# A two-layer hybrid decoder trunk on one core: first weights in halves, warm-up products, squares straight into the ones product, paired output transfers and a new order of issue

## The chip, the cores and the metric

The kernel runs on one core of a Trainium2 chip. Its engines are TensorE (PE; its weight loads are shown as PEld), VectorE (DVE), ScalarE (ACT), GpSimd (POOL) and SyncE (SP), which issues nearly all transfers. The metric is device time in microseconds, the median of the runs of a kernel; lower is better.

## The reference

Two layers. In each, an RMSNorm, one input projection whose columns go to four mixers, an RMSNorm for each mixer's output, an output projection and a residual; then an RMSNorm, a gated FFN and a residual. At the end a last RMSNorm. Everything is float32, the sequence is 1024 long and the model 1024 wide, the FFN 2816.

```python
for l in range(DEPTH):
    h = rmsnorm(x, attn_norm[l])
    proj = h @ w_in[l]
    (c_q, c_kv, k_r, g_b, g_c, u_conv, u_pool,
     q_sw, k_sw, v_sw) = jnp.split(proj, pts, axis=-1)
    y_a = mla_attention(...)        # causal, latent, 4 heads
    y_b = short_gated_conv(...)     # width 3
    y_c = multiscale_pool(...)      # windows 2, 4, 8, 16
    y_d = swa_sink_attention(...)   # window 128, ALiBi, sinks
    groups = jnp.stack([y_a, y_b, y_c, y_d], axis=2)
    gf = groups.astype(jnp.float32)
    gf = gf * lax.rsqrt(jnp.mean(gf * gf, axis=-1, keepdims=True) + RMS_EPS)
    mixed = (gf.reshape(b, s, D_MIX) * mix_norm[l]).astype(x.dtype)
    x = x + mixed @ w_o[l]
    h2 = rmsnorm(x, ffn_norm[l])
    gate, up = jnp.split(h2 @ w_gate_up[l], 2, axis=-1)
    x = x + (jax.nn.silu(gate) * up) @ w_down[l]
return rmsnorm(x, final_norm)
```

## The kernel before

**Layout.** Activations are kept transposed: eight tiles `d` of 128 model channels on the partitions, two halves `t` of 512 positions on the free axis. Every product is made from operands that are split in two: a high part, cast to float32r (`act.copy`, L215 for weights, L283 and L286 elsewhere), and a low part, the rest (`dve.tensor_tensor` with subtract, L216, L284, L287). `mm3` (L272 is its product) adds high by high, high by low and low by high into one PSUM bank, so an output of 128 by 512 over 1024 channels is 24 products. Plain float32 is left in the transposes (L560, L950) and in products with a tile of ones (L336); one with ones is two passes in the trace.

**Stages.** For each layer: the projections of `w_in` and the four mixers with their attention, the output projection, the gate and up products with a Strassen-like scheme over blocks of two by two (`gu_start`, `onto`; `snap`, L1176, copies a partial sum from PSUM between two products onto the same bank; 21 such tiles a layer and one plain one), then the down products in seven combinations of blocks (`B11` to `B22`). In the profile attention and projections of layer 0 are about 50 to 450 us, its FFN 450 to 1050, and the same again for layer 1 until 2008.

**The start.** SP first loads the first weights `w_in[0, 2]`, 128 by 1024 (L207 in `weights`), then in `enter` (L366) the eight tiles of x of one half and later the second weights and the other half. POOL loads `par`, all gains and small parameters (L131). `enter` scales each x tile by its gain on ACT while splitting it (L286, `pcol` reads `par`), and DVE makes the low part (L287). `enter_norm` adds up the squares (`SumSq.add`: Square on ACT, L318, addition on DVE, L324). DVE writes `ones` first of all (L135).

**The end.** In the last layer the block `B22` is done for two column ranges, 0 to 256 and 256 to 512, of the second half of positions; `tail` holds its four accumulations. After each, `evac` adds the bank to x on DVE (L1575), `ss.add` squares and adds it, with the last addition also adding the epsilon (L320). `rnorm` sums over partitions with a product with ones (L336) and takes the inverse root on ACT and DVE (L338 to L344). `finish` scales the eight tiles by gain and norm on DVE (L380) and sends each (L384).

**The order of issue.** `steps_of` makes a list of steps from the program, with what each waits for and its duration in a table of costs. `places` gives each group of instructions its rank plus a shift from the table `MOVES`; `arrange` runs a planner over the list: each engine takes, of what is ready by `SIGNAL` (from the end of a step on one engine until another may use it) and has a buffer that is free (its last use's end and 40 ns), the step of the lowest place. `order_engines` binds the instructions of every engine, SP's transfers too, to the order that comes out.

Of the kernel before, what the change touches and what calls it, by code (L numbers as in the profile page):

```python
# [18 lines left out]
P = 128  # L19
# [92 lines left out]
def trunk_kernel(ctx: ExitStack, tc: tile.TileContext, ins, out):  # L112
# [13 lines left out]
    def rd(ap):  # L126
        return ap.bitcast(F32)


    par = cpool.tile([P, L * PC_N + NK], F32, name="par")  # L130
    pool.dma_start(par, ins["params"])  # L131
# [50 lines left out]

    def tmp(tag="te"):
        return tpool.tile([P, HT], F32, name=tag, tag=tag, bufs={"te": 2, "tn": 3, "tp": 3}[tag])
# [18 lines left out]
    def weights(src, n):  # L203
        if n > 2 * P:
            s = F.pair()
            raw = F.ap2(s)
            sp.dma_start(raw[:, :n], src)  # L207
# [7 lines left out]
        act.copy(hi[:, :n], raw[:, :n])  # L215
        dve.tensor_tensor(out=lo[:, :n], in0=raw[:, :n], in1=rd(hi[:, :n]), op=ALU.subtract)  # L216
# [81 lines left out]
    class SumSq:  # L298
# [7 lines left out]
        def add(self, t, f, cols=whole):  # L306
# [12 lines left out]
            if m == self.n // P:  # L319
# [6 lines left out]
        def rnorm(self, t, cols=whole, tag="t", parts=False):  # L326
# [8 lines left out]
            else:  # L335
                pe.matmul(p, ones, a, start=True, stop=True)  # L336
# [24 lines left out]

    def enter(t):

        for k in range(NK):
            s = xf[k][t] = F.half()
            sp.dma_start(F.ap(s), x_in[k, :, t * HT : (t + 1) * HT])  # L366
            hh[k][t] = half_split(F.ap(s), pcol(0, PC_ATTN + k))

    def enter_norm(t):
# [3 lines left out]
        ratt[t] = ss.rnorm(t, parts=True)  # L373

# [10 lines left out]

    last_silu = None
    for l in range(L):
# [1251 lines left out]
        for cols in (slice(0, 256), slice(256, HT)) if last else ():  # L1639
            for m, p, w in tail:  # L1640
# [64 lines left out]
DRAM_TILES = {"xs", "xp", "xr", "qd", "out"} | {f"ad{n}" for n in range(7)}  # L1705
# [112 lines left out]
def arrange(steps, rank=lambda v: v.rank):  # L1818
# [29 lines left out]
    def takes(v, t):  # L1848
        for name in (x for x in v.tiles if x not in live):
            tag = name.rsplit("_", 1)[0]  # L1850
            if queue[tag][0] != name or tag in held_by or not freed[tag] or freed[tag][0] + 40 > t:
                return False
        return True

    while any(now.values()) or any(later.values()):
# [23 lines left out]
        for name in (x for x in v.tiles if x not in live):  # L1879
# [5 lines left out]
            if freed[tag][0] + 40 > t:  # L1885
                wait = max(wait or 0, freed[tag][0] + 40)
# [289 lines left out]
```

## Time and profile before

| what | value |
|---|---|
| time, median of 3 runs | 2057.77 us (2057.12 to 2057.89) |
| the profiled execution's own time | 2056.9 us |
| its span (first to last instruction) | 2055.1 us |
| PE busy | 2031.7 us (99%) |
| PEld, DVE, ACT busy | 1669.6, 1616.3, 991.3 us |
| moved by DMA | 289.74 MB, 141 GB/s in the mean |

A busy TensorE is not one at its peak: its products are pipelined and the ends are modelled, so the pace of products and the waits of the weight loads say more than the busy share. A row of a timeline gives the start and length in us, engine, line, operation, what is written from what, and how many; a bracket gives the idle time ahead of it and what ended it. A row of waits gives who waited for whom: us in total, times, longest. A row of a landing gives a transfer's size and the us from issue to landing.

### The profile page before, as it was taken

Reading aid. Unit: us, or ns where it says so; the run is one execution under the profiler, and the core shown is the slowest. Engines: PE = TensorE matmul, PEld = TensorE weight load, DVE = VectorE, ACT = ScalarE, POOL = GpSimd, SP = SyncE. Lnnn points to the kernel's source line nnn. Section 1 sums busy time; section 2 is a strip of 40 time slices with the busy share of each in tenths; the row PEclk is TensorE's granted clock in tenths of the full one; section 3 lists DMA queues with packets and bytes.
Section 4 is the critical chain, followed back from the end, with each engine's and each line's share of the span. In section 5 each row is a group of like instructions: output and inputs, shape, how many; then the busy total and the mean of one; then the engine's idle time right before and its main releaser. Section 6 shows DMA issues by size and latency. Waiting matters only on the chain.

```text
span 2055.1 us, 26087 instructions
## 1 busy us (share of the span) xinstructions
PE 2031.7 (99%) x9394; PEld 1669.6 (81%) x9394; DVE 1616.3 (79%) x2872; ACT 991.3 (48%) x1738; POOL 6.7 (0%) x37
## 2 busy tenths in 40 slices
PE   8999999999999999999999999999999999999997
PEld 6887787888888888888888877888788888888887
DVE  7888988997887878655666898889987787786555
ACT  7447657653333335444443576667433333355342
POOL 0000000000000000000000000000000000000000
PEclk9999999999999999999999999999999999999999
DMA  4110222344544447866401102232553444497552
GB/s 182 34 52 31 74 97 86 135 142 161 188 145 170 161 145 259 297 212 207 147 36 44 47 14 90 94 104 97 185 186 139 165 172 144 154 317 271 196 178 83
DMA packets 148817, 289.74 MB, mean 141 GB/s; under 512 B 12608, under 2 KB 72000, under 8 KB 148688
## 3 DMA queue, kind: packets, MB, share of 16 engines
q1 hardware_dynamic: 148656, 288.03, 40.5%
q8 instruction: 74, 1.21, 0.2%
q14 instruction: 55, 0.45, 0.1%
q0 software_dynamic: 32, 0.04, 0.0%
HBM read 204.66 MB, written 83.36 MB: 140 GB/s over the span
## 4 chain that ended last, share of the span: by engine, by line
PE 92%; DVE 3%; ACT 2%; DMA 1%; issue 1%; SPq 0%; DVEq 0%; ACTq 0%
PE ps_mm L272 36%; PE ps_s L272 29%; PE ps_t L272 11%; PE ps_pv L272 8%; PE ps_pv L962 1%; PE ps_t L950 1%; PE ps_s L896 1%; PE ps_t L336 1%; PE ps_pv L572 1%; PE ps_s L898 1%; PE ps_s L897 1%; DMA u<-in_w_o 1%; PE ps_s L511 1%; PE ps_mm L770 1%; DVE u L324 1%
## 5 line engine op out<-in xcount | busy, mean ns | idle before, releaser
L272 PE MATMUL ps_mm<-u,u 128*128 128x512 f32 (+1 forms) x3426 | 855.2, 390 | 10.6 <-ACT u L286 7.2
L272 PEld LDWEIGHTS ps_mm<-u,u 128*128 128x128 f32 x3426 | 629.0, 189 | 140.6 <-ACT u L286 7.2
L272 PE MATMUL ps_s<-u,u 128*128 128x512 f32 x2676 | 646.5, 390 | 0.4 <-ACT u L283 0.4
L272 PEld LDWEIGHTS ps_s<-u,u 128*128 128x128 f32 x2676 | 501.1, 188 | 107.8 <-ACT tn L1176 1.9
L283 ACT CAST u<-u 128x1024 fp32r<-128x1024 f32 (+2 forms) x388 | 335.9, 889 | 392.6 <-PE ps_s L272 85.6
L284 DVE TENSOR_TENSOR u<-u,u 128x1024 fp32r<-128x1024 f32 (+2 forms) x388 | 389.4, 1020 | 148.2 <-ACT u L283 122.4
L272 PE MATMUL ps_t<-u,u 128*128 128x512 f32 (+1 forms) x1118 | 265.3, 378 | 0.0
L272 PEld LDWEIGHTS ps_t<-u,u 128*128 128x128 f32 x1118 | 202.7, 188 | 39.0 <-issue 0.5
L272 PE MATMUL ps_pv<-u,u 128*128 128x512 f32 x696 | 172.0, 390 | 0.0
L272 PEld LDWEIGHTS ps_pv<-u,u 128*128 128x128 f32 x696 | 130.3, 188 | 27.9 <-ACT tn L1176 0.6
L1316 ACT ACTIVATE tp<-tp 128x512 f32<-128x512 f32 x84 | 53.0, 632 | 146.7 <-DVE tp L348 146.5
L283 ACT CAST u<-ps_t 128x512 fp32r<-128x512 f32 (+4 forms) x136 | 64.8, 506 | 73.7 <-PE ps_t L560 35.6
L286 ACT ACTIVATE u<-u,par 128x512 fp32r<-128x512 f32 x100 | 69.2, 718 | 51.9 <-DVE u L1575 16.0
L284 DVE TENSOR_TENSOR u<-ps_t,u 128x512 fp32r<-128x512 f32 (+4 forms) x136 | 76.2, 582 | 14.1 <-ACT u L283 13.6
L1176 ACT COPY tn<-ps_s 128x512 f32<-128x512 f32 x66 | 38.4, 582 | 90.0 <-PE ps_s L272 89.2
L287 DVE SCALAR_TENSOR_TENSOR u<-u,par,u 128x512 fp32r<-128x512 f32 x100 | 73.1, 748 | 9.3 <-ACT u L286 8.8
L161 DVE TENSOR_TENSOR u<-u 128x256 f32<-128x256 f32 x176 | 73.8, 421 | 3.7 <-DMA u<-in_w_dn 1.7
L318 ACT ACTIVATE tn<-u 128x512 f32<-128x512 f32 (+1 forms) x93 | 53.1, 590 | 35.3 <-DVE u L1575 31.8
L216 DVE TENSOR_TENSOR u<-u,u 128x1024 fp32r<-128x1024 f32 (+1 forms) x46 | 51.9, 1129 | 22.4 <-ACT u L215 12.7
L1317 DVE TENSOR_TENSOR tp<-tp,u 128x512 f32<-128x512 f32 x84 | 57.6, 688 | 13.0 <-ACT tp L1316 12.2
L348 DVE TENSOR_TENSOR tp<-tp,u 128x512 f32<-128x512 f32 x80 | 54.8, 688 | 1.3
L215 ACT CAST u<-u 128x1024 fp32r<-128x1024 f32 (+1 forms) x46 | 44.7, 973 | 20.3 <-DMA u<-in_w_in 16.9
(192 smaller groups left out, 2017.9 us busy)
## 6 DMA issues: line engine op xcount, KB each, us to landing
u<-in_w_gu SPq DMA_DIRECT2D x88, 512.0 KB, 3.8
ad<-u SPq DMA_DIRECT2D x154, 256.0 KB, 2.4
u<-ad SPq DMA_DIRECT2D x70, 512.0 KB, 5.2
u<-in_w_dn SPq DMA_DIRECT2D x68, 512.0 KB, 4.1
qd<-u SPq DMA_DIRECT2D x44, 512.0 KB, 3.0
u<-qd SPq DMA_DIRECT2D x32, 512.0 KB, 4.3
u<-in_w_in SPq DMA_DIRECT2D x30, 512.0 KB, 3.5
u<-in_xT SPq DMA_DIRECT2D x32, 256.0 KB, 4.1
```

The costliest lines, as they stand in the source:

```text
L161: dve.tensor_tensor(out=o, in0=o, in1=u, op=ALU.add)
L215: act.copy(hi[:, :n], raw[:, :n])
L216: dve.tensor_tensor(out=lo[:, :n], in0=raw[:, :n], in1=rd(hi[:, :n]), op=ALU.subtract)
L272: pe.matmul(o, w, r, start=start and k == 0 and i == 0, stop=stop and k == n - 1 and i == 2, skip_group_check=again,)
L283: act.copy(hi, f)
L284: dve.tensor_tensor(out=lo, in0=f, in1=rd(hi), op=ALU.subtract)
L286: act.activation(hi, f, AF.Copy, scale=gain)
L287: dve.scalar_tensor_tensor(out=lo, in0=f, scalar=gain, in1=rd(hi), op0=ALU.mult, op1=ALU.subtract)
L318: act.activation(q, f, AF.Square)
L348: dve.tensor_tensor(out=o, in0=a, in1=b, op=ALU.mult)
L1316: last_silu = act.activation(g, g, AF.Silu)
L1317: dve.tensor_tensor(out=g, in0=g, in1=r, op=ALU.mult)
```

## The change

- The first weights, and only these, are loaded and split in two halves of 512 columns. Between the two loads SP issues x tile 0 and the parameters, which were loaded by POOL. `par` is now 128 by 128.
- Ahead of everything TensorE makes eight products of the tile of ones with itself, 128 columns each, into a bank that nobody reads (`warm_up`).
- At the end, in the second column range, the closing addition with the epsilon is made one step earlier, and the last square stays in its own tile and enters the sum as a second product with ones (`also`). The final gains are multiplied in on ACT (`gain`) after the squares; `finish_gained` multiplies by the norm alone into new tiles and sends tiles 0 to 5 in pairs, 6 and 7 alone.
- In the planner's table, what TensorE waits for counts 113 ns more, and so does a buffer that TensorE takes again. `MOVES` is a different table throughout (527 entries before, 456 after).

```diff
-    par = cpool.tile([P, L * PC_N + NK], F32, name="par")
-    pool.dma_start(par, ins["params"])
+    par = cpool.tile([P, P], F32, name="par")
...
+    def warm_up(n):
+
+        p = ps("pv")
+        for _ in range(n):
+            pe.matmul(p[:, :P], ones, ones, start=True, stop=True)
...
-    def weights(src, n):
+    def weights(src, n, between=None):
+        cuts = [slice(0, n // 2), slice(n // 2, n)] if between else [slice(0, n)]
         if n > 2 * P:
             s = F.pair()
             raw = F.ap2(s)
-            sp.dma_start(raw[:, :n], src)
+            for c in cuts:
+                sp.dma_start(raw[:, c], src[:, c])
+                if c is not cuts[-1]:
+                    between()
...
-        act.copy(hi[:, :n], raw[:, :n])
-        dve.tensor_tensor(out=lo[:, :n], in0=raw[:, :n], in1=rd(hi[:, :n]), op=ALU.subtract)
+        for c in cuts:
+            act.copy(hi[:, c], raw[:, c])
+            dve.tensor_tensor(out=lo[:, c], in0=raw[:, c], in1=rd(hi[:, c]), op=ALU.subtract)
...
-                expect(weights, ins["w_in"][l, m], 2 * HT)
+                begin = [first_loads] if (l, m) == (0, 2) else []
+                expect(weights, ins["w_in"][l, m], 2 * HT, *begin)
...
-            if m == self.n // P:
+            if m == self.n // P or closing:
...
-                pe.matmul(p, ones, a, start=True, stop=True)
+                pe.matmul(p, ones, a, start=True, stop=also is None)
+                if also is not None:
+                    pe.matmul(p, ones, also, start=False, stop=True)
...
+    def load_x(k, t):
+        s = xf[k][t] = F.half()
+        sp.dma_start(F.ap(s), x_in[k, :, t * HT : (t + 1) * HT])
+
+    def first_loads():
+        load_x(0, 0)
+        sp.dma_start(par, ins["params"])
...
+    def gain(x, d, t, cols):
+        a = F.ap(x[d][t])[:, cols]
+        act.activation(a, a, AF.Copy, scale=par[:, L * PC_N + d : L * PC_N + d + 1])
+
+    def finish_gained(x, t, cols):
+        r = F.ap(ratt[t])[:, cols]
+        sent = slice(t * HT + cols.start, t * HT + cols.stop)
+        for m in range(NK // 2):
+            o = F.ap2(F.pair()).rearrange("p (b n) -> p b n", b=2)[:, :, cols]
+            both = out[2 * m : 2 * m + 2, :, sent].rearrange("b p n -> p b n")
+            for b in range(2):
+                mul_to(o[:, b], F.ap(x[2 * m + b][t])[:, cols], r)
+                if m == NK // 2 - 1:
+                    sp.dma_start(both[:, b], o[:, b])
+            if m < NK // 2 - 1:
+                sp.dma_start(both, o)
...
+    warm_up(8)
...
         for cols in (slice(0, 256), slice(256, HT)) if last else ():
+            late, q = cols.start > 0, None
...
-                ss.add(1, F.ap(x[2 * m][1])[:, cols], cols)
-            ratt[1] = ss.rnorm(1, cols, tag="s")
-            finish(x, 1, cols)
+                a = F.ap(x[2 * m][1])[:, cols]
+                if late and m == NM - 1:
+                    q = tmp("tn")[:, cols]
+                    act.activation(q, a, AF.Square)
+                else:
+                    ss.add(1, a, cols, late and m == NM - 2)
+                if late:
+                    for d in (2 * m, 2 * m + 1):
+                        gain(x, d, 1, cols)
+            ratt[1] = ss.rnorm(1, cols, tag="s", also=q)
+            (finish_gained if late else finish)(x, 1, cols)
...
-    "DVE": {"PE": 55, "DVE": 33, "ACT": 33, "POOL": 79, "SP": 27},
-    "ACT": {"PE": 52, "DVE": 33, "ACT": 25, "POOL": 77, "SP": 26},
-    "POOL": {"PE": 79, "DVE": 33, "ACT": 32, "POOL": 78, "SP": 27},
-    "SP": {"PE": 50, "DVE": 35, "ACT": 35, "POOL": 80, "SP": 30},
+    "DVE": {"PE": 168, "DVE": 33, "ACT": 33, "POOL": 79, "SP": 27},
+    "ACT": {"PE": 165, "DVE": 33, "ACT": 25, "POOL": 77, "SP": 26},
+    "POOL": {"PE": 192, "DVE": 33, "ACT": 32, "POOL": 78, "SP": 27},
+    "SP": {"PE": 163, "DVE": 35, "ACT": 35, "POOL": 80, "SP": 30},
+REUSE = {"PE": 153, "DVE": 40, "ACT": 40, "POOL": 40, "SP": 40}
...
-            if freed[tag][0] + 40 > t:
-                wait = max(wait or 0, freed[tag][0] + 40)
+            if freed[tag][0] + REUSE[e] > t:
+                wait = max(wait or 0, freed[tag][0] + REUSE[e])
...
 MOVES = {
-    3: -448, 6: -443, 11: -445, 16: -443, 21: -332, 25: -68, 27: -351, 30: -227, 31: -360, 32:
+    3: -428, 4: -411, 5: -410, 8: -366, 10: -349, 12: -409, 13: -350, 15: -125, 17: -414, 22:
...
```

More of the change, by code (lines that the diff above doesn't have):

```diff
@@ L304, in __init__, with add @@
             self.done = {}
-        def add(self, t, f, cols=whole):
+        def add(self, t, f, cols=whole, closing=False):
             e = EPS * self.n / P
@@ L324, in add, with rnorm @@
                 dve.tensor_tensor(out=a, in0=a, in1=q, op=ALU.add)
-        def rnorm(self, t, cols=whole, tag="t", parts=False):
+        def rnorm(self, t, cols=whole, tag="t", parts=False, also=None):
             a, n = F.ap(self.acc[t])[:, cols], self.n
@@ L1702, in areas @@
     return name, [(p, p + dims[0][1], c, c + span)]
-DRAM_TILES = {"xs", "xp", "xr", "qd", "out"} | {f"ad{n}" for n in range(7)}
+DRAM_TILES = {"ws", "xs", "xp", "xr", "qd", "out"} | {f"ad{n}" for n in range(7)}
 BUFS = {"ps_mm": 2, "ps_s": 3, "ps_t": 2, "ps_pv": 1, "te": 2, "tn": 3, "tp": 3, "vraw": 2, "vhi": 2, "vlo": 2, "sm1": 16, "sm2": 16, "sm16": 2}
@@ L1850, in takes @@
             tag = name.rsplit("_", 1)[0]
-            if queue[tag][0] != name or tag in held_by or not freed[tag] or freed[tag][0] + 40 > t:
+            if queue[tag][0] != name or tag in held_by or not freed[tag] or freed[tag][0] + REUSE[e] > t:
                 return False
@@ L2149, in _layout @@
     fin = i["final_norm"].reshape(NK, P).T
-    a["params"] = c(np.concatenate([lay.reshape(P, -1), fin], axis=1))
+    par = np.concatenate([lay.reshape(P, -1), fin], axis=1)
+    a["params"] = c(np.pad(par, ((0, 0), (0, P - par.shape[1]))))
     a["rope_q"], a["rope_k"], a["const"] = _constants()
```

5 lines of the change are left out of this document (3 added, 2 removed), and 113 rows, old and new, of the table MOVES.

## The prediction

> **What bounds the kernel now.** I read the table of engines first, then cut the span into stages by busy time, then read the start and the end instruction by instruction, and last the waits of the two stages between them in which the TensorE is not full.
>
> ```profile
> span 2055.1 us, 26087 instructions
> PE 2031.7 (99%) x9394; PEld 1669.6 (81%) x9394; DVE 1616.3 (79%) x2872; ACT 991.3 (48%) x1738; POOL 6.7 (0%) x37
> ...
> 845.16 14.96 PE ps_t L272 x66
> ```
>
> ```profile
> core 0: us, PE busy (x) PEld busy (x) DVE busy (x) ACT busy (x) POOL busy (x), PEclk, DMA share, GB/s
> 0.00:50.00 50.00, 42.78 (x178) 34.20 (x179) 38.35 (x61) 37.08 (x59) 0.86 (x5) 1.00 0.51 187
> 50.00:450.00 400.00, 397.37 (x1921) 322.57 (x1920) 355.72 (x778) 246.51 (x527) 2.82 (x16) 1.00 0.22 77
> 450.00:1050.00 600.00, 600.00 (x2645) 495.62 (x2644) 441.16 (x631) 241.04 (x325) 0.00 (x0) 1.00 0.54 186
> 1050.00:1450.00 400.00, 397.59 (x1919) 322.60 (x1918) 340.62 (x748) 240.06 (x518) 2.98 (x16) 1.00 0.19 67
> 1450.00:2008.00 558.00, 558.00 (x2458) 460.18 (x2457) 417.58 (x608) 218.00 (x292) 0.00 (x0) 1.00 0.55 192
> 2008.00:2056.00 48.00, 35.98 (x281) 34.46 (x279) 22.83 (x51) 8.66 (x20) 0.00 (x0) 0.90 0.25 88
> ```
>
> The reader is to see that TensorE has no hole in 600 + 558 us (the FFN stages); a run of 66 products there takes 14.96 us, 0.227 us each. No edit removes one of these products, so 1158 us cannot shrink. What can move: the first 50 us (7.2 us without a product), the end (12.0 us without one by the last row, of which 0.9 lie behind the span's end), and the two attention stages, where the visible idle time is only 2.6 and 2.4 us. All four pieces that have a name (split weights, warm-up, squares, paired transfers) touch the start or the end alone; the new order of issue touches everything.
>
> **The change, the start.** The timeline, then landings (each from a window of the DMA view around the issue: x tile 0 and the parameters at 1.2, x tile 7 at 4.69, the second weights at 5.89), then the products' pace in two windows.
>
> ```profile
> 0.74 0.38 SPq L207 DMA_DIRECT2D u<-in_w_in  x1
> 0.84 0.17 DVE L135 MEMSET ones<- 128x128 f32 x1 [0.84 <-PEq L2162]
> ...
> 4.70 1.04 ACT L215 CAST u<-u 128x1024 fp32r<-128x1024 f32 x1 [2.68 <-DMA u<-in_w_in]
> 5.78 1.23 DVE L216 TENSOR_TENSOR u<-u,u 128x1024 fp32r<-128x1024 f32 x1 [4.51 <-ACT u L215]
> ...
> 6.43 1.93 ACT L286 ACTIVATE u<-u,par 128x512 fp32r<-128x512 f32 x3
> ...
> 7.19 8.09 PE L272 MATMUL ps_mm<-u,u 128*128 128x512 f32 x24 [7.19 <-ACT u L286]
> ...
> 11.52 2.07 DVE L287 SCALAR_TENSOR_TENSOR u<-u,par,u 128x512 fp32r<-128x512 f32 x3
> ...
> 13.53 1.03 ACT L215 CAST u<-u 128x1024 fp32r<-128x1024 f32 x1
> ...
> 15.12 0.84 PE L272 MATMUL ps_s<-u,u 128*128 128x512 f32 x3
> ```
>
> ```profile
> u<-in_xT SPq DMA_DIRECT2D x1, 256.0 KB, 4.7
> par<-in_params POOLq DMA_DIRECT2D x1, 43.0 KB, 4.8
> ...
> u<-in_xT SPq DMA_DIRECT2D x1, 256.0 KB, 6.8
> ...
> u<-in_w_in SPq DMA_DIRECT2D x1, 512.0 KB, 6.9
> ```
>
> ```profile
> 7.19:11.19 4.00, 3.98 (x9) 2.80 (x10) 1.00 1.03 399
> 11.90:15.12 3.22, 3.22 (x15) 2.63 (x14) 1.00 1.05 385
> ...
> L336 PE MATMUL ps_s<-u,ones 128*128 128x256 f32 x4 | 1.3, 409 | 1.4 <-DVE u L320 1.4
> ```
>
> The first product waits for x tile 0 (landed 1.18 + 4.7 = 5.88) and its gain, scaled in about 0.7 us (1.93 / 3 and the tail of one). The weights, issued just before, were there at 4.70, so 256 KB more cost 1.18 us. Afterwards the order on SP is half the weights, x tile 0, the parameters, the other half. The first half stands where the weights stood less 1.18 us, at 3.5; x tile 0 at 4.70; the parameters (64 KB, a quarter of 1.18) at 5.0, now from SP instead of POOL, where they took until 1.25 + 4.8 = 6.05. The scaled copy ends at 5.7: first product about 5.75 instead of 7.19, 1.45 us earlier. Half a CAST and half a subtraction (0.55 and 0.65 us) end at 4.7, ahead of it. The two additional issues on SP (0.38 us each) push x tiles 1 to 7 and the second weights back by less than one place, but the bytes in front of them grow by 21 KB only, 0.1 us.
>
> That is not what reaches the next stage. The 24 products of the first weights take 7.9 us although 15 of them later fit into 3.22 us: 0.44 us each in the first window, 0.21 in the second. The warm-up is aimed at this: nine products at 0.2 us too much are 1.9 us. The column PEclk says 1.00 in both windows, so the profile here does not show the reason; the Trainium skill (TensorE: Matmul & The Clock Gate, The HAM clock gate) says that TensorE starts at half its clock and is released by some 3.4 us of activity, in windows that run free of the kernel's start. The eight warm-up products cost two passes of 128 columns each; two passes of 256 columns took 1.3 us for four at most, 0.33 us a pass, so 16 passes of half the width are 2.6 us at that pace and 5.3 us at half pace. They can begin when the ones are written, at about 1.05, so they end between 3.7 and 6.3. Cover: TensorE has nothing to do until 5.75; what they could push back is 0.6 us.
>
> Now the supply. x tile 7 lands at 4.69 + 6.8 = 11.5, afterwards 11.6; its two halves are ready 0.7 and 1.4 us later (ACT, then DVE at 2.07 / 3), and two products after that end at 13.5 instead of 15.12. The second weights land at 5.89 + 6.9 = 12.8, afterwards 12.9; their CAST takes 1.03, so the next block starts at 13.9 at the earliest with SP's order as it is, instead of 15.12: 1.2 us. If the new order of transfers brings the second weights ahead of some x tiles, TensorE has two blocks to work on while x comes in, and the whole 1.45 + 1.9 = 3.3 us can show. I take 1.5 us, near the lower of the two because every byte still comes over the same wire; ends 0.3 (second weights late by two more SP issues) and 3.3.
>
> One rule speaks against this piece. The DMA view moved 399 and 385 GB/s in those two windows. The Trainium skill (DMA: Bandwidth & Descriptors, Rules for kernel authors) advises against cutting a transfer, since both parts share the same 16 engines and small ones pay overhead; the trace agrees that the wire is full (shares of 1.03 and 1.05). By that rule the start would give only the order of arrival; it is the third rival.
>
> **The end.**
>
> ```profile
> 2043.00 0.28 PE L272 MATMUL ps_mm<-u,u 128*128 128x256 f32 x1
> 2043.32 0.42 DVE L1575 TENSOR_TENSOR u<-u,ps_mm 128x256 f32<-128x256 f32 x1
> 2043.66 0.42 DVE L324 TENSOR_TENSOR u<-u,tn 128x256 f32<-128x256 f32 x1
> 2043.78 0.42 ACT L318 ACTIVATE tn<-u 128x256 f32<-128x256 f32 x1 [3.43 <-DVE u L1575]
> 2044.22 0.43 DVE L320 SCALAR_TENSOR_TENSOR u<-tn,u 128x256 f32<-128x256 f32 x1
> 2044.70 0.70 PE L336 MATMUL ps_s<-u,ones 128*128 128x256 f32 x2 [1.42 <-DVE u L320]
> ...
> 2047.80 3.26 DVE L380 SCALAR_TENSOR_TENSOR u<-u,par,u 128x256 f32<-128x256 f32 x8
> ...
> 2048.31 3.77 SPq L384 DMA_DIRECT2D out<-u  x8
> ```
>
> This is one chain: last product, evacuation, square, addition, product of ones, norm, eight scalings, eight transfers. The change lets the square go to the product of ones directly, so the addition and its handing over, 2044.22 to 2044.70, go: 0.48 us. It adds a second product of ones (0.70 us for its two passes), of which the first may run as soon as the sum of the other squares is closed. Here the addition before last ends at 2044.08, so that product would run from 2044.1 to 2044.8 and the new one behind it, with its first load hidden, 0.4 to 0.7 more: 2045.2 to 2045.4 against 2045.40 now. If the new order has that addition earlier (DVE is filled until 2043.06 by the first half's scalings), the full 0.48. I take 0.35, ends 0 and 0.48. The eight gains move from the last scalings to ACT, at 0.42 us each by L318; ACT waits 3.43 us just ahead, so seven are free, and the last one (it must follow the square) lies under the product of ones. The scaling itself stays one DVE pass over 256 columns (L380: 3.26 / 8 = 0.41; L324: 0.42): nothing. Then SP: eight issues take 3.77 us, 0.49 apart, while DVE delivers every 0.40; the last issue begins 3.9 us after the first scaling. With three paired and two single transfers SP has time between, and the last goes at most one issue after the last scaling: 3.4 to 3.5. Gain 0.4; ends 0.1 (two blocks in one transfer cost SP more) and 0.5. The end together: 0.75, from 0.1 to 1.0.
>
> **The order of issue.** The planner's table now charges 113 ns more for a result that TensorE waits for and for a bank that it takes again, and all the shifts are new. What TensorE loses to such waits is seen better in its weight loads than in its products, since the ends of products are modelled: in 50 to 450 us 25 rows that are not "issue" add up to 13.1 us in 44 waits, in 1050 to 1450 us 22 rows to 13.2 us in 45. First and last row of each, and from the chain a run of 33 products of 256 columns:
>
> ```profile
> PEld ps_mm L272 <- ACT u L215: 1.5, 2, 1.1
> ...
> PEld ps_t L333 <- DVE u L284: 0.2, 1, 0.2
> ...
> PEld ps_pv L962 <- DVE u L284: 1.4, 7, 0.2
> ...
> PEld ps_s L896 <- ACT u L283: 0.2, 1, 0.2
> ...
> 2019.10 3.96 PE ps_mm L272 x33
> ```
>
> A load can hide behind the product before it for 0.227 us less its own 0.12 (a load accompanies every 256-column product, and 33 of these take 3.96 us), 0.107 us a wait; so 26.3 - 89 x 0.107 = 16.8 us are really lost. That is the ceiling of any order. A planner that knows of the additional 0.11 us can hide the short waits; the long ones (1.1 us in a row above) come from transfers and from DVE, whose prices are unchanged, and are dealt out anew. Nothing in the trace says how well the new order does. I take 3.0 us, less than a fifth of the ceiling; ends 9 better and 5 worse.
>
> **Sum.** 1.5 + 0.75 + 3.0 = 5.25 us. The profiled execution took 2056.9 us (span 2055.1 and 1.8 around it), so 2051.65 for such a run; the median of the runs, 2057.77, is 0.9 above it, so 2052.5.
>
> **The rivals.** First, the new order gives nothing: the waits are dealt out anew with the same total. For it: 17 of the 26.3 us cannot come from the 113 ns alone. Then 2.25 us are left: 2055.5. Second, slower: the order that suits attention puts waits into the full stages. There every gate-and-up tile of the FFN copies a partial sum out (L1176) between two products onto the same bank, and those copies already hold up loads:
>
> ```profile
> PEld ps_s L272 <- ACT tn L1176: 1.9, 9, 0.2
> ```
>
> A wait of 0.2 us and a load of 0.12 that is no longer hidden are 0.32 us. With one more in each of the 42 tiles it is 13.4 us: 2057.77 - 2.25 + 13.4 = 2068.9. It decides from 20 such waits on (2.25 + 4.1 = 6.35 us). Against it: the two FFN stages have DVE at 74% and ACT at 39 to 40%, so there is room. Third, the supply holds the start (the rule above): 0.3 + 0.75 + 3.0 = 4.05 us, 2053.7.
>
> **How the numbers follow.** What a measurement of this kernel can tell from no change is about 0.2%, 4.1 us. The forecast, 2052.5, gets 0.62; it counts as faster. The first rival gets 0.21 and the third 0.07: within 0.2%, 0.28. The second gets 0.10. The range, 2046.5 to 2057.0, takes in the first and third rival and the order's gain up to about 9 us; left out are the slower case and gains above 11 us.
>
> **What would show it.** Right: TensorE's first product from tiles at 5.5 to 6 us, its pace 0.23 us from the start, the second block before 14.2 us; a second product of ones at the end and 0.6 us less from the last product to the end of the span; the loads' waits in the attention stages clearly below 26 us. Wrong: a first pace of 0.44 again; a product of ones that waits for the closing addition; holes in the two full stages; or attention stages as long as before.

## The result: 7.3 us faster, with a start that is longer, not shorter

| | before | after |
|---|---|---|
| time, median | 2057.12 us (2055.78 to 2057.93, 7 runs) | 2049.83 us (2048.81 to 2051.5, 7 runs) |
| profiled execution, its span | 2056.9, 2055.1 us | 2050.61, 2048.5 us |

The ratio is 0.9965, with a 95% interval from 0.9954 to 0.9977: 0.35% faster. The line numbers have moved: the products of `mm3` are now at L283 (L272 before), the scaled copy of x at L297 (L286), the cast of weights at L225 (L215), `LDWEIGHTS` is shown as PEld as before.

To see where 6.6 us of span went, the two traces were laid beside each other at equal work: the time at which TensorE had streamed the same number of columns (warm-up left out).

| place (time in before) | after minus before, us | in the stretch |
|---|---|---|
| 22 us | +2.5 | start: +2.5 |
| layer 0's FFN, middle (1025) | +0.9 | layer 0's attention: -1.6 |
| layer 1's FFN (1641) to its last product | -4.8 | layer 1's attention: -5.7 |
| span's end (2055.1) | -6.6 | end: -1.8 |

The start, forecast 1.5 us shorter, is 2.5 longer. The end and the attention stages gave more than forecast. A row for one stage from one trace is not good to a tenth: in the ten traces with the new order, this one and those of nine runs below, layer 0's attention is 0.7 to 2.8 us shorter than before and layer 1's 4.4 to 6.0, both together (22 to 1641 us) 6.2 to 8.7. The cut into stages (columns as in the prediction's) shows the two full stages without a change of substance and TensorE's clock below 1.00 in the first 50 us:

```profile
core 0: us, PE busy (x) PEld busy (x) DVE busy (x) ACT busy (x) POOL busy (x), PEclk, DMA share, GB/s
0.00:50.00 50.00, 44.86 (x183) 36.81 (x184) 34.87 (x56) 34.26 (x55) 0.20 (x4) 0.93 0.50 187
...
450.00:1050.00 600.00, 598.90 (x2643) 495.38 (x2642) 441.44 (x631) 242.06 (x325) 0.00 (x0) 1.00 0.54 185
1050.00:1450.00 400.00, 398.55 (x1941) 327.63 (x1940) 344.19 (x754) 244.18 (x522) 3.21 (x16) 1.00 0.19 68
1450.00:2002.00 552.00, 552.00 (x2436) 456.73 (x2435) 413.12 (x600) 215.96 (x290) 0.00 (x0) 1.00 0.56 194
```

The start of after, from the timeline:

```profile
0.73 0.87 SPq L214 DMA_DIRECT2D u<-in_w_in  x2
...
1.05 3.78 PE L186 MATMUL ps_pv<-ones 128*128 128x128 f32 x16 [1.05 <-DVE ones L134]
1.65 0.42 SPq L377 DMA_DIRECT2D u<-in_xT  x1
2.12 0.43 SPq L381 DMA_DIRECT2D par<-in_params  x1
...
6.37 0.63 ACT L324 ACTIVATE u<-u 128x512 f32<-128x512 f32 x1 [1.51 <-DMA u<-in_xT]
6.99 0.17 DVE L502 TENSOR_SCALAR nsink<-par 128x4 f32<-128x4 f32 x1 [1.42 <-DMA par<-in_params]
...
7.62 0.63 ACT L329 ACTIVATE tn<-u 128x512 f32<-128x512 f32 x1 [0.63 <-DMA u<-in_xT]
8.16 3.77 ACT L297 ACTIVATE u<-u,par 128x512 fp32r<-128x512 f32 x6
...
8.92 7.51 PE L283 MATMUL ps_mm<-u,u 128*128 128x512 f32 x18 [4.09 <-ACT u L297]
...
16.26 0.86 PE L283 MATMUL ps_s<-u,u 128*128 128x512 f32 x3
```

Three things went otherwise than reckoned. SP issues both halves of the weights ahead of x tile 0: the planner decides the order of transfers, not the source. On ACT two squares (L324 and L329, the second waiting for x tile 1) stand ahead of the first scaled copy. So the first product from tiles comes at 8.92, after 4.09 us without work. And in that gap TensorE loses its clock, as four stretches of the trace show (the third number from the end is the granted clock, PEclk):

```profile
8.00:8.40 0.40, 0.00 (x0) 0.00 (x0) 0.12 (x1) 0.40 (x2) 0.00 (x0) 0.99 1.08 343
8.40:8.80 0.40, 0.00 (x0) 0.00 (x0) 0.40 (x1) 0.40 (x2) 0.00 (x0) 0.50 1.03 358
14.80:15.20 0.40, 0.40 (x2) 0.30 (x2) 0.40 (x1) 0.40 (x2) 0.00 (x0) 0.50 1.04 399
15.20:15.60 0.40, 0.40 (x3) 0.31 (x3) 0.40 (x2) 0.40 (x2) 0.00 (x0) 0.97 1.04 399
```

It falls to half at 8.4 us, half a microsecond before the first product, and comes back at 15.2: 6.8 us at half, with 0.43 us a product. The trace's list of clock changes begins with a rise at 4.98, just after the warm-up's end at 4.83; its 16 passes had all taken 0.21 us or more. The second block starts at 16.26 instead of 15.12.

The loads' waits in the attention stages, first and last row that is not "issue" of 50 to 450 us and of 1050 to 1450 us:

```profile
PEld ps_s L936 <- ACT u L294: 2.0, 2, 1.8
...
PEld ps_t L527 <- DVE te L361: 0.2, 1, 0.2
```

```profile
PEld ps_pv L612 <- ACT u L294: 0.7, 3, 0.3
...
PEld ps_pv L1002 <- DVE u L295: 0.2, 1, 0.2
```

16 rows with 9.0 us in 21 waits, and 15 rows with 4.9 us in 18. Before it was 26.3 us in 89 waits, now 13.9 in 39. By the prediction's own formula (0.107 us of each wait is hidden) 9.7 us are really lost instead of 16.8: 7.1 us less, which is the size of what the attention stages gave. It also fits by stage: 1.6 and 5.4 us less by the formula, 1.6 and 5.7 at equal work.

The end:

```profile
2039.01 0.42 ACT L1691 ACTIVATE tn<-u 128x256 f32<-128x256 f32 x1 [1.07 <-DVE u L1615]
...
2039.47 0.70 PE L349 MATMUL ps_s<-tn,ones 128*128 128x256 f32 x2 [0.53 <-ACT tn L1691]
2040.21 0.38 ACT L351 ACTIVATE tn<-ps_s 128x256 f32<-128x256 f32 x1 [0.25 <-PE ps_s L349]
...
2042.51 2.77 DVE L361 TENSOR_TENSOR u<-u,u 128x256 f32<-128x256 f32 x8
2042.96 0.81 SPq L410 DMA_DIRECT2D out<-u  x2
2043.97 1.71 SPq L412 DMA_DIRECT2D out<-u  x3
```

From the last product of tiles (it ends at 2038.51; before at 2043.28) to the first logarithm (L351; L338 before) it is 1.70 us instead of 2.22, and from the first scaling (L361; L380 before) to the span's end 6.0 instead of 7.3. The scaling, now a product of two tensors, takes 2.77 / 8 = 0.35 us each instead of 0.41. The plan sends the two single tiles first (L410) and the three pairs last (L412), the last of them 0.03 us after the last scaling.

### The profile page after: what moved, and what is told of

It is laid out like the page before. It is cut to its first block, busy times and chain, and to the rows that moved or that the text cites. A ratio compares the mean times of both kernels' runs of the same rounds, so it can differ in the third digit from the quotient of the medians.

```text
span 2048.5 us, 26170 instructions
## 1 busy us (share of the span) xinstructions
PE 2028.9 (99%) x9412; PEld 1678.4 (82%) x9412; DVE 1616.6 (79%) x2872; ACT 996.1 (49%) x1747; POOL 7.0 (0%) x36
## 4 chain that ended last, share of the span: by engine, by line
PE 94%; DVE 3%; ACT 1%; DMA 1%; issue 0%; SPq 0%; DVEq 0%; ACTq 0%
PE ps_mm L283 37%; PE ps_s L283 29%; PE ps_t L283 11%; PE ps_pv L283 8%; PE ps_pv L1002 2%; PE ps_t L990 1%; PE ps_s L936 1%; PE ps_s L938 1%; PE ps_s L937 1%; PE ps_t L347 1%; PE ps_pv L612 1%; PE ps_s L551 1%; PE ps_mm L810 1%; PE ps_t L600 1%; DVE u L295 1%
## 5 line engine op out<-in xcount | busy, mean ns | idle before, releaser
L283 PE MATMUL ps_mm<-u,u 128*128 128x512 f32 (+1 forms) x3426 | 858.4, 389 | 5.3 <-ACT u L297 4.1
L283 PEld LDWEIGHTS ps_mm<-u,u 128*128 128x128 f32 x3426 | 631.0, 189 | 135.2 <-ACT u L297 4.4
L283 PE MATMUL ps_s<-u,u 128*128 128x512 f32 x2676 | 655.5, 389 | 0.6 <-DVE u L295 0.4
L283 PEld LDWEIGHTS ps_s<-u,u 128*128 128x128 f32 x2676 | 501.8, 188 | 106.0 <-DVE u L295 0.9
L294 ACT CAST u<-u 128x1024 fp32r<-128x1024 f32 (+2 forms) x388 | 335.8, 890 | 393.0 <-PE ps_s L283 71.8
L295 DVE TENSOR_TENSOR u<-u,u 128x1024 fp32r<-128x1024 f32 (+2 forms) x388 | 389.3, 1020 | 135.7 <-ACT u L294 110.4
L283 PE MATMUL ps_t<-u,u 128*128 128x512 f32 (+1 forms) x1118 | 268.5, 378 | 2.0 <-ACT u L294 1.1
L283 PEld LDWEIGHTS ps_t<-u,u 128*128 128x128 f32 x1118 | 203.1, 188 | 42.0 <-issue 1.8
L283 PE MATMUL ps_pv<-u,u 128*128 128x512 f32 x696 | 165.6, 389 | 0.0
L283 PEld LDWEIGHTS ps_pv<-u,u 128*128 128x128 f32 x696 | 130.6, 188 | 27.1
L297 ACT ACTIVATE u<-u,par 128x512 fp32r<-128x512 f32 x100 | 68.8, 717 | 60.5 <-DVE u L1615 23.4
L295 DVE TENSOR_TENSOR u<-ps_t,u 128x512 fp32r<-128x512 f32 (+4 forms) x136 | 76.5, 583 | 12.6 <-ACT u L294 11.9
L329 ACT ACTIVATE tn<-u 128x512 f32<-128x512 f32 (+1 forms) x92 | 52.4, 592 | 36.9 <-DVE u L1615 28.5
L226 DVE TENSOR_TENSOR u<-u,u 128x1024 fp32r<-128x1024 f32 (+2 forms) x47 | 51.9, 1107 | 14.2 <-PE ps_mm L283 4.8
L361 DVE TENSOR_TENSOR tp<-tp,u 128x512 f32<-128x512 f32 x80 | 55.2, 690 | 1.6
L225 ACT CAST u<-u 128x1024 fp32r<-128x1024 f32 (+2 forms) x47 | 44.9, 957 | 23.5 <-DMA u<-in_w_in 18.6
```

The source lines that it names most:

```text
L225: act.copy(hi[:, c], raw[:, c])
L226: dve.tensor_tensor(out=lo[:, c], in0=raw[:, c], in1=rd(hi[:, c]), op=ALU.subtract)
L283: pe.matmul(o, w, r, start=start and k == 0 and i == 0, stop=stop and k == n - 1 and i == 2, skip_group_check=again,)
L294: act.copy(hi, f)
L295: dve.tensor_tensor(out=lo, in0=f, in1=rd(hi), op=ALU.subtract)
L297: act.activation(hi, f, AF.Copy, scale=gain)
```

## The experiments

**The order of issue, in three runs.** Theory: the gain is the new order's; rival: it is that of the start and the end.

`order_alone`: the kernel before with both tables of after, the shifts put on the same groups of instructions.

```diff
-SIGNAL = {...}; 40 ns for every buffer
+SIGNAL = {...}; REUSE = {"PE": 153, ...}   # after's
-MOVES = {...}
+MOVES = {...}                              # after's, on before's groups
```

> The kernel before with the new costs and the new shifts alone (shifts of the steps that it does not have are left out, the end keeps its own). Theory: the new order is what shortened the attention stages (7.3 us between the traces), so 2057.1 - 7 = 2050 us, within 1.5; the waits of the weight loads in the two attention stages fall from 26 to about 14 us; the start is within 0.7 us of the one before. Rival, the four named pieces brought the gain: 2056 to 2058 us, waits as before.

Measured: 2050.42 us (2050.19 to 2051.1), ratio 0.9971 [0.996, 0.9983]. At equal work it is 0.4 us behind before at 22 us and 6.6 ahead after layer 1's attention. By the medians the order alone carries 6.3 us. Its waits of loads fell to 16.3 us in 42, not to the 14 us expected; by the formula that is 5.0 us less, where equal work shows 7.0 from 22 us on. So the formula gives the size, not the tenth.

`costs_alone`: the same without the new shifts.

```diff
+SIGNAL, REUSE of after; MOVES as before
```

> The kernel before with the new costs (113 ns more for what TensorE waits for and takes again) and its old shifts. If the costs carry the gain: 2050 to 2053 us. If it is the search that carries it, old shifts under other costs are as good as or worse than before: 2056 to 2062 us. I hold the second for likelier, two to one.

Measured: 2084.23 us, ratio 1.0136 [1.0122, 1.015].

`shifts_alone`: the same without the new costs.

```diff
+MOVES of after; SIGNAL and the 40 ns as before
```

> The kernel before with the new shifts of the planner's due times (MOVES), its old costs, old start and old end: the counterpart of the run with the new costs alone (2084 us). Theory (shifts are corrections found for one set of costs; with another the plan is another, and neither half carries the gain): 10 to 30 us slower than before, 2067 to 2087. Rival (the shifts are the gain, the costs only helped the search to find it): 2050 to 2054.

Measured: 2071.74 us, ratio 1.0074 [1.006, 1.0087]. Either half does harm: a table of shifts belongs to the costs under which it was searched. So the 113 ns are not a gain by themselves. Part of the harm is the clock again; two stretches of `costs_alone` in layer 0's attention:

```profile
356.17:359.58 3.41, 1.39 (x7) 0.81 (x5) 2.06 (x4) 1.60 (x3) 0.23 (x2) 1.00 0.20 66
...
359.60:366.40 6.80, 3.25 (x9) 2.13 (x10) 2.76 (x4) 4.22 (x8) 0.00 (x0) 0.51 0.00 0
```

A stretch of 3.4 us in which TensorE was busy for 1.39 is followed by 6.8 us at half clock. Two more such stretches begin at 370.0 and 445.1 us. TensorE was busy for 3.5, 4.6 and 5.8 us of the three, so the half clock cost at most half of this, 7 of the 23 us that layer 0's attention lost; the rest are waits.

**The parts without the order.** `parts_alone`: after with before's costs and shifts (the end keeps after's shifts), and the first transfers as the source has them.

```diff
-SIGNAL, REUSE, MOVES of after
+SIGNAL, MOVES of before; REUSE = 40 for all
+    3: -448, 4: -448, 5: -448,   # half weights, x tile 0, parameters, other half
```

> The kernel after with the old costs and shifts (the end keeps the new shifts; the first weights, x tile 0 and the parameters are issued in the order of the source). Theory: the end brings 1.8 us, the start 1 to 1.5 us now that no square stands ahead of the first scaled copy, the attention stages nothing: 2054 us, within 1. First product from tiles at 6 to 6.6 us at 0.23 us each. Rival, split weights and warm-up cost time by themselves (as the start of the kernel after seems to say): the start is 2 us later than before, 2057.5 us.

Measured: 2060.24 us (2059.04 to 2063.01), ratio 1.002 [1.001, 1.0029]: slower than before, and the theory that start and end give 2 to 3 us fell. It is beyond the rival's 2057.5 too. Its timeline:

```profile
4.71 0.24 DVE L502 TENSOR_SCALAR nffn<-par 128x8 f32<-128x8 f32 x2
...
7.09 0.62 ACT L225 CAST u<-u 128x512 fp32r<-128x512 f32 x1 [2.23 <-DMA u<-in_w_in]
7.62 2.56 ACT L297 ACTIVATE u<-u,par 128x512 fp32r<-128x512 f32 x4
...
8.39 8.24 PE L283 MATMUL ps_mm<-u,u 128*128 128x512 f32 x25 [3.55 <-ACT u L297]
```

The parameters are there by 4.71, but the scaled copies stand on ACT behind the cast of the second half, which lands only at 7.09, 5 us after its issue. The trace's first clock change is a rise at 12.87: here the eight products had not raised the clock at all. At 22 us this kernel is 3.4 us behind before.

**The start, in six runs.** Theory: after's start lost 2.5 us because TensorE idled after a warm-up that was too short, and its clock fell back; rival: the supply sets the second block, whatever the clock does.

`warm24`: after, with more warm-up; the planner is given the price of 8, so that the length of the warm-up changes no order (as in all these runs).

```diff
-    warm_up(8)
+    warm_up(24)
```

> The kernel after with 24 warm-up products instead of 8, the order of every engine unchanged. Theory: in the kernel after the warm-up ends at 4.8 us and the first product comes at 8.9, so the granted clock falls back to half at 9.2 and the first 13 products take 0.43 us each; with 24 the gap closes (11 at 0.43 us until 5.8, 13 at 0.21 until 8.6), the first products run at 0.23 us and the second block starts 2 us earlier: 2047.8 us, within 0.8. Rival, the supply of x tiles holds this stage: 2049.3 to 2050.3 us, no change. Third, the ones keep TensorE beyond 8.9 us: later by up to 1 us.

Measured: 2047.16 us (2045.84 to 2048.09), ratio 0.9956 [0.9943, 0.9968].

```profile
1.05 7.25 PE L186 MATMUL ps_pv<-ones 128*128 128x128 f32 x48 [1.05 <-DVE ones L134]
...
8.71 0.50 PE L283 MATMUL ps_mm<-u,u 128*128 128x512 f32 x1 [0.41 <-ACT u L297]
9.50 4.18 PE L283 MATMUL ps_mm<-u,u 128*128 128x512 f32 x17 [0.29 <-DVE u L298]
...
13.51 0.85 PE L283 MATMUL ps_s<-u,u 128*128 128x512 f32 x3
```

The first product comes 0.2 us earlier than in after, the second block 2.75 us, and at 22 us it stands exactly where before stands. The clock rose during the warm-up, at 4.49, and held.

`warm1`: `warm_up(1)`.

> After with one warm-up product instead of eight, the order of every engine as in after. Theory (eight end so early that the clock falls back before the tiles come, so they are worth nothing): first product from tiles at 8.4 to 8.9 as in after, 0.43 us each until the clock rises 3.4 to 5 us behind it, second block at 15 to 16.3; 2049.0 to 2050.5, within 1 us of after's 2049.8. Rival (even a clock that falls back has saved something): 1 to 2 us slower than after, 2051 to 2052.

Measured: 2050.04 us (2049.85 to 2051.07), ratio 0.997 [0.9958, 0.9981]. First product at 8.98, second block at 16.05; at 22 us 2.3 behind before. By the medians eight warm-up products are worth nothing that can be measured. The traces are not so clear: after's own start is as late as this one, but two other executions with eight and the same first steps (`tail_single` and `tail_square` below) stand 1.6 and 1.8 us ahead of it.

`start_order`: after with the first steps' order written by hand, as the prediction reckoned with it.

```diff
+HEAD = {"SP": [half weights, x tile 0, parameters, other half],
+        "ACT": [cast, scaled copy, scaled copy, cast of the other half, ..., squares], "DVE": [...]}
...
+            queue = queue[:at] + [rank[r] for r in HEAD[e]] + rest
```

> After, with only the first steps' order set by hand to the one that the prediction reckoned with: on SyncE half of the weights, x tile 0, the parameters, the other half; on ScalarE the first scaled copies ahead of the squares and ahead of the second half's cast; all later orders as in after. Theory (what after lost at its start was lost by the order of its first steps: the scaled copy stood behind two squares, TensorE idled 4.1 us after its warm-up and its clock fell back): x tile 0 lands at about 4.3, the parameters at 4.7, first product from tiles at 5.5 to 6.0 instead of 8.92, less than 1.2 us after the warm-up, so the clock holds: pace 0.23, start 3 to 4 us earlier than after's, 2045.8 to 2046.8. Rival 1 (eight warm-up products are too few to lift the clock): the first product comes as early, but at 0.43 us each, and the second block at 14.5 to 15.5: 2048 to 2049. Rival 2 (the first microseconds are bound by the wire): the second half of the weights lands at 7 us or later and everything behind it with it; the second block stays at 16: 2049.8.

Measured: 2049.72 us (2048.67 to 2050.07), ratio 0.9962 [0.9948, 0.9975].

```profile
1.66 0.42 SPq L381 DMA_DIRECT2D par<-in_params  x1
...
6.52 0.17 DVE L502 TENSOR_SCALAR nsink<-par 128x4 f32<-128x4 f32 x1 [1.73 <-DMA par<-in_params]
...
6.59 0.72 ACT L297 ACTIVATE u<-u,par 128x512 fp32r<-128x512 f32 x1 [2.52 <-DMA par<-in_params]
...
7.36 7.57 PE L283 MATMUL ps_mm<-u,u 128*128 128x512 f32 x18 [2.53 <-ACT u L297]
...
14.77 1.19 PE L283 MATMUL ps_s<-u,u 128*128 128x512 f32 x3
```

With the very order of the prediction the first product comes at 7.36, not at 5.75: the scaled copy waits for the parameters, which land 4.8 us after their issue. The first 18 products took 7.57 us, so the clock was down here too; its first recorded change is a rise at 13.73, and the pace goes from 0.43 to 0.23 us there. Eight products had not raised it. At 22 us it is 1.5 us behind before. The theory's time was missed. Rival 2's time fits, though its second block (14.8) does not; the pace and the second block are those of rival 1, that eight are too few to lift the clock.

`start_order_warm16`: the same with `warm_up(16)`.

> start_order with 16 warm-up products instead of 8. Theory: the warm-up ends between 6.2 (if the clock rises on the way) and 7.9; the first product follows at once at 0.23 us: 2045.8 to 2046.8, and not slower than start_order by more than 0.5 us. By rival 1 it is 2 us faster than start_order (2046 to 2047 against 2048 to 2049); by rival 2 the pace is 0.23 but the second block still starts at 16: 2049 to 2050.

Measured: 2051.77 us (2048.95 to 2052.6), ratio 0.9971 [0.9961, 0.9981]. TensorE now runs its first products in 0.23 us and then waits: x tile 1 lands at 8.47. At 22 us it is 1.6 us behind, as without the longer warm-up: with the halves in this order the supply decides. Why its median lies 2 us above that of `start_order` was not found; the traces differ by 0.8 us, in layer 0's attention.

`whole_warm18`: after without the split, the parameters from GpSimd as before, 18 warm-up products; order and end new.

```diff
-                begin = [first_loads] if (l, m) == (0, 2) else []
-                expect(weights, ins["w_in"][l, m], 2 * HT, *begin)
+                expect(weights, ins["w_in"][l, m], 2 * HT)
-            if (k, t) != (0, 0):
-                load_x(k, t)
+            load_x(k, t)
+    pool.dma_start(par, ins["params"])
-    warm_up(8)
+    warm_up(18)
```

> After without the split of the first weights: weights whole, x tile 0 behind them, the parameters from GpSimd as before (so the start of order_alone), but with 18 warm-up products and the new end. Theory (the start gains by the clock alone, and the split gains nothing): warm-up ends between 6.6 and 7.2, first product at 7.2 as before, now at 0.23 us instead of 0.44; the second block starts at 13.8 to 14.6 instead of 15.1, and with the end's 1.8 us and the order's 6.6: 2046.5 to 2047.8. Rival (the split and the early x tile 0 are worth what the prediction gave them, 1.2 to 1.5 us, once the clock is up): start_order_warm16 is faster than this one by 1 us or more. Rival 2 (the supply alone sets the second block): second block at 15.1, 2048.6.

Measured: 2047.32 us (2046.83 to 2049.64), ratio 0.9954 [0.9941, 0.9966].

`whole_warm8`: the same with `warm_up(8)`.

> whole_warm18 with 8 warm-up products as in after: weights whole, parameters from GpSimd, order and end new, so only the split of after and its order of first transfers are undone. Theory (with the old first transfers the supply sets the second block, and the clock decides little; the split costs, since it brings the first product from 7.2 to 8.9): first product at 7.2 to 7.9, second block at 13.5 to 15.1; order_alone's 2050.4 less the end's 1.8: 2048.6, from 2047.5 to 2049.2. Rival (the clock after eight products decides, whole or split): it falls back at about 9 us, the second block comes at 16, and the time is after's, 2049.8 to 2050.5.

Measured: 2048.42 us (2047.31 to 2049.47), ratio 0.9961 [0.9947, 0.9974]. First product at 7.26, second block at 14.16. From `whole_warm18`, timeline and two stretches:

```profile
7.90 2.71 PE L283 MATMUL ps_mm<-u,u 128*128 128x512 f32 x10
...
10.89 2.11 PE L283 MATMUL ps_mm<-u,u 128*128 128x512 f32 x8 [0.28 <-DVE u L298]
...
13.11 1.12 PE L283 MATMUL ps_s<-u,u 128*128 128x512 f32 x3
```

```profile
11.00:13.00 2.00, 2.00 (x8) 1.31 (x8) 2.00 (x6) 2.00 (x5) 0.00 (x0) 1.00 1.06 408
13.00:15.00 2.00, 1.67 (x5) 0.89 (x6) 2.00 (x3) 2.00 (x5) 0.00 (x0) 1.00 1.05 406
```

The second block starts 2 us earlier than before, but at 22 us the kernel is 0.1 us behind before: after 13 us TensorE, at full pace, waits for what comes in, and the wire (share 1.05 to 1.06, over 400 GB/s) is full. Without the split eight products do nearly as well (0.4 behind at 22 us), although in `whole_warm8` the clock rose only at 12.59. And `order_alone`, with the whole weights and no warm-up at all, is 0.4 behind too: with whole weights the warm-up is worth 0.3 us by these traces. So of after's four combinations of split or whole, short or long warm-up, three stand within 0.4 us of before at 22 us; only split with short falls behind.

How far is a matter of the execution: `tail_single` and `tail_square` below have after's first steps unchanged, and their traces are 0.7 and 0.5 us behind, after's own is 2.5. In all three the clock rose at 4.8 to 5.0 us and fell at 8.2 to 8.4; in these two it was back at 11.9 and 11.6, in after only at 15.2. From 12 to 16 us, `tail_single` first, then after:

```profile
12.00:16.00 4.00, 4.00 (x19) 3.29 (x18) 4.00 (x6) 4.00 (x7) 0.00 (x0) 1.00 1.05 405
```

```profile
12.00:16.00 4.00, 4.00 (x12) 3.18 (x11) 4.00 (x7) 4.00 (x7) 0.00 (x0) 0.60 1.06 407
```

**The end, in two runs.** Theory: the queue of issues on SP sets the end, so the pairs bring it; rival: the faster multiplication brings 0.5 us by itself.

`tail_single`: after with eight single transfers.

```diff
-                if m == NK // 2 - 1:
-                    sp.dma_start(both[:, b], o[:, b])
-            if m < NK // 2 - 1:
-                sp.dma_start(both, o)
+                sp.dma_start(both[:, b], o[:, b])
```

> After, with the last eight results of the second half sent one by one, each as soon as it is multiplied, instead of three pairs and two single ones; squares, gains and multiplications as in after. Theory (at the end the queue of issues on SyncE bounds, not the multiplication): eight issues of 0.47 us follow one another as in the kernel before, the last begins 3.8 us after the first multiplication instead of 2.6; from there to the span's end 7.2 us instead of 6.0: 2051.0, and the faster multiplication (0.346 instead of 0.41 us) is worth nothing without the pairs. Rival (the multiplication carries 0.5 us of it): 6.7 us, 2050.5.

Measured: 2050.05 us (2049.01 to 2050.42), ratio 0.9965 [0.9951, 0.9978].

`tail_square`: after with the direct square, but with the old `finish`.

```diff
-                if late:
-                    for d in (2 * m, 2 * m + 1):
-                        gain(x, d, 1, cols)
-            (finish_gained if late else finish)(x, 1, cols)
+            finish(x, 1, cols)
```

> After with the direct square and the second product of ones, but with the old scaling (gain in the same pass on VectorE, 0.41 us each) and eight single transfers. Theory (the end's gain of 1.8 us is 0.5 of the square and 1.3 of the outputs, and of these 0.8 are the pairs, by the run that sends one by one): last product to first logarithm 1.7 us as in after, first scaling to the span's end 7.3 us as before instead of 6.0: 1.3 us slower than after, 2051.1. By the prediction's terms (outputs 0.4): 2050.2.

Measured: 2050.67 us (2048.72 to 2051.26), ratio 0.9969 [0.9959, 0.998]. The times of both are within the scatter of after; their traces tell more. `tail_single`:

```profile
2041.51 2.77 DVE L361 TENSOR_TENSOR u<-u,u 128x256 f32<-128x256 f32 x8
2041.96 3.82 SPq L409 DMA_DIRECT2D out<-u  x8
```

`tail_square`:

```profile
2041.62 3.25 DVE L419 SCALAR_TENSOR_TENSOR u<-u,par,u 128x256 f32<-128x256 f32 x8
2042.14 3.82 SPq L423 DMA_DIRECT2D out<-u  x8
```

Eight issues take 3.82 us in both, whether a scaling takes 0.35 or 0.41 us, and from the first scaling to the span's end (2048.3 and 2048.4) both need 6.8 us. The faster multiplication alone is worth nothing; with the pairs it is 6.0. The 7.2 and 7.3 us expected were missed, because 7.3 was one execution of before: `order_alone`, with the same old end, needs 6.9 (2041.21 to 2048.1).

**The best version.** `warm24` (2047.16) and `whole_warm18` (2047.32) both beat before by 0.44 to 0.46%, where after beats it by 0.35%. Their medians lie 2.5 to 2.7 us below after's, which ran on another chip (before's medians there and here were 2056.7 to 2057.5); the intervals of the ratios overlap with after's, so that this gain rests on the traces of the start as much as on the times. Between the two no difference was measured.

## Why the prediction was right in total and wrong in its terms

It said 2052.5 within 2046.5 to 2057.0; 2049.83 came. It was right that it would be faster, and that the full stages would hold and the attention stages give most. But of three terms one had the wrong sign and two were too small. That the total came out near is in part luck: the start was missed by 4.0 us one way, the order by 4.3 and the end by 1.05 the other.

| term | forecast | by the traces |
|---|---|---|
| start | -1.5 | +2.5 (+0.5 and +0.7 in two other executions) |
| order of issue | -3.0 | -7.3 (-6.2 to -8.7 in all ten) |
| end | -0.75 | -1.8 |

Of its own signs of being right, those of the start failed: the first product came at 8.92 instead of 5.5 to 6, at 0.43 us instead of 0.23, and the second block at 16.26 instead of before 14.2. A first pace of 0.44 was one of its signs of being wrong. Those of the end and of the loads' waits came.

**The start.** Four steps failed. First, "afterwards the order on SP is half the weights, x tile 0, the parameters, the other half" read the order of the source; transfers are steps of the planner like all others, and its new shifts put both halves first. Second, "scaled in about 0.7 us" left out what stands ahead of the scaled copy on ACT. Before has a square there as well, which starts when x tile 0 has landed and ends at 6.53:

```profile
5.90 0.63 ACT L313 ACTIVATE u<-u 128x512 f32<-128x512 f32 x1 [0.15 <-DMA u<-in_xT]
```

From the landing at 5.88 to the first product at 7.19 it was 1.3 us, not 0.7, and in after there are two squares. Third, "the parameters (64 KB, a quarter of 1.18) at 5.0" reckoned landings by bytes in the order of issue. The first half came as reckoned (3.4 to 3.5 against 3.5), the parameters at 6.5 to 7.0 in after and `start_order`, but by 4.71 in `parts_alone`, which has the same first four issues as `start_order`: a transfer in a queue of several doesn't always land by its share of bytes. Fourth, the warm-up's cover: "TensorE has nothing to do until 5.75; what they could push back is 0.6". The question was not how far a warm-up pushes the products back, but whether it raises the clock and how long TensorE idles after it. Of six traces with eight products three show no rise before 12.5 us (`parts_alone`, `start_order`, `whole_warm8`); in the other three it rose as the warm-up ended and fell again in the gap. With 16, 18 and 24 it rose during the warm-up, at 6.8, 7.0 and 4.5 us. The prediction cited the Trainium skill (TensorE: Matmul & The Clock Gate, The HAM clock gate) for the release of the clock; the same section says that an idle window of about 3.4 us throttles it again. The trace agrees (0.99 to 0.50 at 8.4 us, 3.6 us after the last warm-up product), and this half of the rule should have been weighed.

The third rival, that the supply holds the start, was right in substance: with the clock up and the weights whole TensorE is 1.4 us ahead of before at 11.6 us, and at 22 us nothing of it is left. No run with the halves stands ahead of before at 22 us by more than 0.01 us. The rule of the Trainium skill that the prediction set beside this rival (DMA: Bandwidth & Descriptors, Rules for kernel authors) speaks of halves by partitions, these were halves by columns. Whether cutting costs anything the runs don't decide: with a long warm-up the halves (`warm24`) and the whole weights (`whole_warm18`) lie 0.14 us apart there, and with a short one after's first steps changed with the split.

**The order.** The mechanism and the way to read it were right: waits of loads, less 0.107 us each. The term was mis-sized: "less than a fifth of the ceiling" of 16.8 us, where 7.1 us came by the same formula, 42%; in `order_alone` it was 5.0. The first rival's argument, that the 113 ns can't bring it, was true and beside the point: `costs_alone` lost 27 us, and only with shifts searched under the new costs is there a gain. What in the trace of before could have told how far the search would get stays open.

**The end.** The direct square brought 0.52 us, not 0.35: the sum of the other squares was closed early enough, the prediction's upper case. "The scaling itself stays one DVE pass over 256 columns: nothing" was wrong in the duration (0.35 for a product of two tensors, 0.41 for the one with a scalar) but right in the worth, since SP sets the pace of single transfers. The pairs brought 0.8 us against single transfers, where 0.4 was forecast: "the last goes at most one issue after the last scaling" gave 3.4 to 3.5 from the first scaling to the last issue; with the faster scaling it is 2.8 (2045.31 after 2042.51). The remaining 0.4 to 0.5 us lie between the old end in before and the old end in `order_alone` and `tail_square`, with the same old scaling and single transfers, so they are taken as scatter.

## What to carry to other kernels

A warm-up must last until the real work starts: ask whether it raises the clock and how long the engine idles after it, not only what it delays. It pays only as far as the supply keeps up; with whole weights it was 0.3 us here. Where a planner sets the order of transfers, read the order of issue from its plan, and don't reckon landings by adding up bytes. A table of searched shifts and the costs it was searched with are one thing: neither is worth anything alone, and added waits can cost more than their length when they let the clock fall while there is work.

## What the runs showed of the hardware

- TensorE's clock falls within a kernel, not only ahead of it: in the kernel after it falls 3.6 us into a gap of 4.09 us (for 6.8 us, in `tail_single` with the same first steps for 3.4). In `costs_alone` it falls after 3.4 us with 1.39 us of work, so not only after idling.
- The same eight warm-up products, busy for 3.8 us, raised the clock in three of six traces (at 4.8 to 5.0 us) and not in the other three.
- The column of the granted clock says 1.00 up to its first recorded change, whatever the pace is: in `warm1` this is a rise at 14.69 us. `warm1` ran six products in this stretch, as many as after did at a granted 0.50:

```profile
9.30:12.00 2.70, 2.70 (x6) 1.83 (x6) 2.70 (x5) 2.70 (x6) 0.00 (x0) 1.00 1.01 401
```

```profile
9.30:12.00 2.70, 2.70 (x6) 1.83 (x6) 2.70 (x5) 2.70 (x6) 0.00 (x0) 0.50 1.03 407
```

The first line is `warm1`, the second after. The prediction's remark that the profile of before doesn't show the reason for 0.44 us a product is explained by it: before's clock was at half as well, by its pace, and the first change in its trace is a rise at 11.75 us, where its products go from 0.43 to 0.23 us.
- The same transfer of 64 KB, third in the same queue and issued at 1.66, landed by 4.71 in one execution and at 6.52 in another.
